# One fused decoder trunk on one core: eight weight sums in another place, a decay computed in another split, and the first weights loaded in two halves

## The chip, the core and the metric

The kernel runs on one core of a Trainium2 chip. A core has five engines with queues of their own: TensorE (PE, matrix products), VectorE (DVE), ScalarE (ACT), GpSimd (POOL) and SyncE (SP, which here only issues DMA transfers); sixteen DMA engines move data between the memory of the chip and the core's own. Each engine works through its instructions in the order of the program and waits, where it must, for the others' semaphores. The metric is the device time of one execution in microseconds, the median of several runs.

## What is computed

Two layers on a sequence of 1024 rows of width 1024, all in fp32. Layer 0 mixes the rows by a gated delta rule (8 heads of width 128, chunks), layer 1 by a state-space model; in both a memory attention runs beside the mixer, one output projection joins the two, and an MLP with squared ReLU follows. The reference, cut:

```python
for i in range(DEPTH):                      # DEPTH = 2
    if i % 2 == 0:
        mix, xq = gdn_mixer(x, gdn_w_in[j], ...)
    else:
        mix, xq = s5_mixer(x, s5_w_in[j], ...)
    cross = memory_attention(xq, mem, w_kv_mem[i])
    h = jnp.concatenate([mix, cross], axis=-1) @ w_o[i]
    x = layer_norm(DN_ALPHA * x + h, ln1_g[i], ln1_b[i])
    f = jnp.square(jax.nn.relu(x @ mlp_w1[i])) @ mlp_w2[i]
    x = layer_norm(DN_ALPHA * x + f, ln2_g[i], ln2_b[i])
```

In the delta rule the part that the change touches is the decay of a chunk, `exp(gc_i - gc_j)` below the diagonal and 0 above it, where gc is the running sum of the gates.

## The kernel before

**Products.** Every large fp32 product is three fast products (`mm3`, lines 397 to 399): each operand is split into a high part (a cast on ScalarE) and a low part (the rest, a subtraction on VectorE), and TensorE adds high*high, high*low and low*high. The small products of the delta rule run in plain fp32. In the profile `wih` and `wil` are the two parts of a weight, `xTh` and `xTl` those of x^T, and so on.

**Stages.** Up to about 30 us x^T comes in sixteen pieces of 256 KB, and the first weight (`w_in[8]`, the keys of head 0) in one load of 512 KB behind the first piece and the small gate weights `wba`; each is cast as it arrives (`load_xT`, `gdn_load_x`). From 30 to 210 us come the keys of two heads, the memory's keys and values and the memory attention. From 210 to 620 us run seven heads of the delta rule (`run`): for head h the recurrence `gdn_recur(h)` is woven into `gdn_fill(h + 1)`, the projections and the triangular inverses of the next heads. A step of the recurrence is a chain through three engines: `ks` (PE, L1452), R (DVE, L1454), `pe` (PE, L1458), e (ACT, L1460), `pS` (PE, L1464), S (DVE, L1469), and again. After half of its eight steps the output `po` is scaled: squares on ACT (L1478), a square root on POOL (L1480), the scaling `on` on ACT (L1483), and only then may `po` be written again (L1455). For every second head `gdn_inverse` puts a block of sixteen operations on VectorE (L1260 and L1262) for the inverses of the next two. From 600 to 790 us the last recurrence and the output projection run (`out_stream`: operands `so` from loads `or`, products `tm`), with the layer norm and the transposes of its rows (`block_end`: `y`, `tw`, `xB`) at the end. From 790 us the MLP: `mlp_first` with 16 pairs of blocks, and beside it (`side`) the tables of layer 1's state-space model. Then layer 1 in the same stages.

**Sums for the MLP.** The MLP's first product multiplies blocks by a scheme with seven products in place of eight, and needs sums of weight blocks. For the first four pairs of each layer the sums are made ahead: `weight_sums(i, n)` loads four 128x512 blocks, makes four sums on VectorE (`left_sums`, L640 to L643) and stores them in `wsd` (L645), from where `mlp_weights` (L696) loads them later. The same helpers serve `out_sums` and `head_sums`, for the output projection.

**Order.** The program is traced in the order of the source, and then `settle` reorders all engines by a list scheduler with its own costs: each instruction gets a due time, an engine takes what can run and is due first, and TensorE may be reordered within a reach of 40 us. Instructions made under `aside` are due at the latest 50 us after their place in the source. The number of buffers of a tag (`TAGS`: five of h5, nine of h2) bounds how early a load can be placed. `self.begin` names the last instruction that stays in the order of the source.

Of the kernel before, what the change touches and what calls it, by code (L numbers as in the profile page):

```python
# [33 lines left out]
class Trunk:  # L34
# [620 lines left out]
        for q, o in enumerate((a, d, b, c)):  # L655
            self.nc.sync.dma_start(dst[q], o)

    def weight_sums(self, i, n):

        w = [self.a["w1"][i, 2 * n + q] for q in range(2)]  # L660
        self.left_sums([w[q][:, x * HALF:(x + 1) * HALF] for q in range(2) for x in range(2)], self.wsd[i, n])

    def head_sums(self, p, tag="h5"):

# [139 lines left out]
    def mlp_first(self, i, B, ahead, side):  # L804

        held = []
        O = self.mlp_weights(i, 0, not ahead)
        for n in range(16):
            nxt = []
            self.mlp_pair(n, O, B, ahead, held, lambda: nxt.append(self.mlp_weights(i, n + 1, n + 1 >= 4) if n < 15 else None))  # L810
            O = nxt[0]
            for fb in {2: (0,), 4: (1,), 6: (2,), 8: (3,), 10: (4,), 11: (5,), 13: (6,), 15: (7,)}.get(n, ()) if side else ():
                side(fb, ("pa",) * 4)
        self.finish(held)
        self.finish(held)

# [171 lines left out]
    def load_xT(self, wba):  # L988

        nc = self.nc  # L990
        raw = self.quad(F32, "x") + self.quad(F32, "x")
        nc.sync.dma_start(raw[0][:, 0:HALF], self.a["xT"][0:P, 0:HALF])
        nc.sync.dma_start(wba, self.a["wba"])
        r0 = self.load_raw(self.a["w_in"][8], "wir")
        xT = self.new_xT()

        def take(k, h):
            s = raw[k][:, h * HALF:(h + 1) * HALF]
            hi, lo = xT[h][0][:, k, :], xT[h][1][:, k, :]
            nc.scalar.copy(hi, s)  # L1000
            nc.vector.tensor_tensor(lo, s, f32(hi), op=ALU.subtract)

        take(0, 0)
        self.begin = nc.cur_bb.bb.instructions[-1]
        w0 = tuple(self.tile("w1", [P, 1024], F32R, "wi" + q) for q in "hl")
        for c in range(2):
            c = slice(c * HALF, (c + 1) * HALF)
            nc.scalar.copy(w0[0][:, c], r0[:, c])  # L1008
            nc.vector.tensor_tensor(w0[1][:, c], r0[:, c], f32(w0[0][:, c]), op=ALU.subtract)  # L1009
        for h in range(2):  # L1010
            for k in range(KT):
                if k or h:
                    nc.sync.dma_start(raw[k][:, h * HALF:(h + 1) * HALF], self.a["xT"][k * P:(k + 1) * P, h * HALF:(h + 1) * HALF])
        nc.sync.dma_start(self.cw, self.a["cw"])
        nc.sync.dma_start(self.ng, self.a["ng"])
        nc.gpsimd.tensor_scalar(self.ng, self.ng, 0.5, None, op0=ALU.mult)
        nc.sync.dma_start(self.dsk, self.a["dskT"])
        for k in range(KT):
            for h in range(2):
                if k or h:  # L1020
                    take(k, h)
        return xT, w0

    def gdn_load_x(self):

        nc = self.nc
        wba = self.tile("h1", [P, KT * 16], F32, "wba")
        xT, w0 = self.load_xT(wba)
        wt = self.tile("h1", [P, KT, 2, 16], F32R, "wbah")
        wv = wba.rearrange("p (k c) -> p k c", k=KT)  # L1030
        nc.scalar.copy(wt[:, :, 0, :], wv)
        nc.vector.tensor_tensor(wt[:, :, 1, :], wv, f32(wt[:, :, 0, :]), op=ALU.subtract)
        ba = self.tile("h1", [P, 8, 16], F32, "ba")
        pt = self.psum("pa", "bat", (P, 8, 32))
        for h in range(2):
            ps = self.psum(("po", "sc")[h], "ba")
            for k in range(KT):
                nc.tensor.matmul(ps[:32, :], wt[:, k].rearrange("p s c -> p (s c)"), xT[h][0][:, k, :], start=k == 0, stop=False)
                nc.tensor.matmul(ps[:16, :], wt[:, k, 0, :], xT[h][1][:, k, :], start=False, stop=k == KT - 1)
            bt = self.tile("h1", [P, HALF], F32, "baT")  # L1040
            nc.vector.tensor_copy(bt[:32, :], ps[:32, :])
            for j in range(4):
                nc.tensor.transpose(pt[:, 4 * h + j, :], bt[:32, j * P:(j + 1) * P], self.ident[:32, :32])
        nc.vector.tensor_copy(ba, pt[:, :, 0:16])
        nc.vector.tensor_tensor(ba, pt[:, :, 16:32], ba, op=ALU.add)
        self.gates(ba)
        return xT, w0
# [92 lines left out]
    def decay(self, h, hf, tag):  # L1140

        nc = self.nc
        pb = self.sums(h, hf, tag)
        d = self.tile(tag, [P, 4, P], F32, "D")
        for t in range(4):
            nc.vector.scalar_tensor_tensor(d[:, t, :], pb[:, t, :], self.ngc[:, 4 * hf + t, h:h + 1], self.maskneg, op0=ALU.add, op1=ALU.add)
        nc.scalar.activation(d, d, AF.Exp)
        return d

    def gdn_keys(self, h, xT, w=None):  # L1150
# [1080 lines left out]
    def run(self):  # L2231
        nc = self.nc
        a = self.a
        d = lambda n, shape: self.dp.tile(shape, F32, tag=n, name=n)
        dsk = self.const("dsk", [P, 64])
        self.dsk, self.same = dsk[:, 0:8], dsk[:, 8:24]
        self.rouse(8)
        self.gdn_consts()
        nc.vector.tensor_reduce(self.same, self.ident.rearrange("p (g o) -> p o g", o=16), axis=AX.X, op=ALU.add)
        self.s5_scratch()  # L2240

        self.cat = d("cat0", [1536, T])
        xT, w0 = self.gdn_load_x()
        self.kTs = self.quad(F32, "kT")
        self.TT, self.qT, self.qe, self.vT, self.zs, self.outs = {}, {}, {}, {}, {}, []
        for h in range(2):
            for _ in self.gdn_keys(h, xT, (w0, None)[h]):
                pass
            for hf in range(2):
                self.gdn_keys_out(h, hf)  # L2250
        self.gdn_inverse(0)
        kv = []
        for _ in self.mem_kv(0, kv, False):
            pass
        tags = ("h4", "h3", "h2", "h2", "h2")
        fill = self.gdn_fill(0, xT, 30.0)
        self.memory_heads(xT, kv, tags, fill)
        self.mix = self.quad(F32, "mix")
        self.take(fill, 1e9)
        self.wsd = d("wsd", [2, 4, 4, P, HALF])  # L2260
        self.osd = d("osd0", [5, 4, P, HALF])
        self.wods = [d("wod0", [5, 4, P, HALF]), d("wod1", [5, 4, P, HALF])]
        sums = {"m": self.weight_sums, "o": self.out_sums, "p": self.out_sums, "h": self.head_sums}
        for h in range(7):
            for x in {0: "h0 h1", 1: "m00 m01 m02 o00", 2: "m03 o01", 3: "h2 o02 o03 m10", 4: "o04 m11", 5: "h3 m12", 6: "m13"}.get(h, "").split():
                self.aside(sums[x[0]], *map(int, x[1:]))
            fill = self.gdn_fill(h + 1, xT, 34.0 if h % 2 else 0.0)
            self.weave(self.gdn_recur(h), fill, 2.75 if h < 5 else 1.95)
            self.take(fill, 1e9)
        self.head_sums(4, "h2")  # L2270
        x = a["x"].rearrange("(n s) d -> s n d", s=8)
        y = self.rows(x)
        self.x1 = d("x1", [8, P, T])
        self.x2 = d("x2", [8, P, T])
        self.x3 = d("x3", [8, P, T])
        self.hd = d("hd", [16, 7, P, HALF])
        steps, B, ahead = self.block_end(0, y, self.x1)
        stream = iter(lambda: next(steps), None)
        self.weave(self.gdn_recur(7), stream, 2.25)
        self.take(stream, 8.0)  # L2280
        self.gdn_out_last()
        for _ in stream:
            pass
        for _ in steps:
            pass

        self.cat = d("cat1", [1536, T])
        self.osd = d("osd1", [5, 4, P, HALF])

        def u_front(xT):  # L2290
            self.s5t = self.tile("xT", [P, 4 * T], F32, "s5t")
            self.us = [self.s5_u(m, xT) for m in range(2)]
            for u in self.us:
                next(u)
                yield

        xT = self.mlp_block(0, B, ahead, self.x1, self.s5_side, self.x2, u_front)
        for u in self.us:
            next(u)
        self.s5_front(xT)  # L2300
        y = self.rows(self.x2)
        steps, B, ahead = self.block_end(1, y, self.x3)
        for _ in steps:
            pass
        self.mlp_block(1, B, ahead, self.x3, None, a["out"].rearrange("(n s) d -> s n d", s=8), None)
        self.settle(self.begin, self.nc.cur_bb.bb.instructions[-1], reach=40.0, ahead=70.0, margin=0.2, late=0.7)
# [169 lines left out]
```

## Time and profile before

| | us |
|---|---|
| median of 3 runs | 2501.73 |
| lowest, highest | 2500.79, 2506.34 |
| the profiled execution | 2501.58 |
| its span, first to last instruction | 2499.7 |
| TensorE busy in the span | 2465.4 |
| VectorE, ScalarE, GpSimd busy | 1963.5, 1286.1, 435.2 |

The profile is of one execution. Its span is 1.9 us shorter than that execution's time. An engine is busy while it has an instruction in hand; an idle time carries the name of what ended it. TensorE's instructions overlap, so two of them start closer together than one takes. The chain of waits follows the program back from the last instruction, at each step to what released it.

### The profile page before, as it was taken

To read this page: it belongs to the slowest core of one execution; us is meant where nothing else is said; L and a number is where in the kernel's file an instruction comes from. 1 tells how busy PE (TensorE), PEld (TensorE's weight loads), DVE (VectorE), ACT (ScalarE), POOL (GpSimd) and SP (SyncE) were. 2 spreads that over 40 slices of the span, in tenths; PEclk is the share of its full clock that TensorE was granted. 3 is DMA by queue.
4 is the path that set the end of the run, shared out by engine and by line. 5 is a ranking of instruction groups with operands and counts; after the bars stand their busy time and mean duration, and the time that the engine had idled before them with its cause. 6 is when DMAs were issued, how large, how long until landed. Compare 5 with 4: busy or idle time off the path is not lost.

```text
span 2499.7 us, 36835 instructions
## 1 busy us (share of the span) xinstructions
PE 2465.4 (99%) x12133; PEld 2057.0 (82%) x12133; DVE 1963.5 (79%) x3655; ACT 1286.1 (51%) x2738; POOL 435.2 (17%) x675
## 2 busy tenths in 40 slices
PE   9999999999999999999999999999999999999998
PEld 7888887888887888878888888888887888888886
DVE  8786888777778798879988967786687666578778
ACT  6555555545456566554444244564365555544442
POOL 1242333313002033212211123111021000000001
PEclk9999999999999999999999999999999999999999
DMA  6453585768754576586454489669736444674532
GB/s 224 110 171 119 140 265 141 233 183 245 258 173 155 187 234 219 178 284 234 142 161 147 153 249 312 197 224 328 255 126 210 148 144 164 228 250 129 170 104 97
DMA packets 317167, 480.63 MB, mean 192 GB/s; under 512 B 105728, under 2 KB 136656, under 8 KB 316976
## 3 DMA queue, kind: packets, MB, share of 16 engines
q1 hardware_dynamic: 289456, 423.23, 51.5%
q0 software_dynamic: 25216, 50.86, 6.9%
q10 hardware_dynamic: 2304, 4.20, 0.4%
q8 instruction: 95, 1.56, 0.2%
q14 instruction: 96, 0.79, 0.1%
HBM read 321.39 MB, written 156.73 MB: 191 GB/s over the span
## 4 chain that ended last, share of the span: by engine, by line
PE 90%; DVE 5%; DMA 2%; ACT 2%; issue 1%; POOL 1%; SPq 0%; POOLq 0%; DVEq 0%; ACTq 0%
PE q L398 7%; PE q L399 7%; PE q L397 7%; PE pA L397 4%; PE pA L399 4%; PE pA L398 4%; PE tm L397 4%; PE tm L399 4%; PE tm L398 4%; PE wi L397 3%; PE wi L398 3%; PE wi L399 3%; PE pC L399 2%; PE pC L397 2%; PE pC L398 2%; PE pB L397 2%
## 5 line engine op out<-in xcount | busy, mean ns | idle before, releaser
L397 PE MATMUL q<-wkh,hkh 128*128 128x512 f32 x784 | 306.4, 391 | 1.2 <-ACT G L1909 1.2
L398 PE MATMUL q<-wkl,hkh 128*128 128x512 f32 x784 | 305.9, 390 | 0.4 <-DVE wkl L911 0.4
L399 PE MATMUL q<-wkh,hkl 128*128 128x512 f32 x784 | 305.4, 390 | 0.0
L910 ACT CAST wkh<-wr 128x512 fp32r<-128x512 f32 x168 | 104.8, 624 | 240.0 <-PE q L398 189.4
L521 POOL TENSOR_TENSOR mv<-mv,mhalf 128x1 f32<-128x1 f32 x32 | 27.9, 873 | 858.3 <-DVE mv L515 584.2
L397 PEld LDWEIGHTS q<-wkh,hkh 128*128 128x128 f32 x784 | 147.2, 188 | 32.8 <-ACT G L1909 2.1
L398 PEld LDWEIGHTS q<-wkl,hkh 128*128 128x128 f32 x784 | 147.3, 188 | 31.0 <-DVE wkl L911 1.1
L399 PEld LDWEIGHTS q<-wkh,hkl 128*128 128x128 f32 x784 | 147.2, 188 | 30.4
L911 DVE TENSOR_TENSOR wkl<-wr,wkh 128x512 fp32r<-128x512 f32 x168 | 116.0, 690 | 67.1 <-issue 57.7
L397 PE MATMUL wi<-xTh,wih 128*128 128x512 f32 x384 | 159.4, 415 | 1.5 <-ACT wih L1008 1.5
L399 PE MATMUL wi<-xTh,wil 128*128 128x512 f32 x384 | 152.6, 397 | 0.0
L398 PE MATMUL wi<-xTl,wih 128*128 128x512 f32 x384 | 151.7, 395 | 0.0
L911 DVE TENSOR_TENSOR hkl<-hr,hkh 128x512 fp32r<-128x512 f32 x196 | 134.8, 688 | 0.0
L910 ACT CAST hkh<-hr 128x512 fp32r<-128x512 f32 x196 | 120.8, 616 | 0.1
L397 PE MATMUL tm<-so 128*128 128x512 f32 x280 | 109.8, 397 | 0.1
L1644 ACT CAST so<-or 128x1024 fp32r<-128x1024 f32 x70 | 71.8, 1049 | 69.1 <-DMA or<-wod 47.1
L1645 DVE TENSOR_TENSOR so<-or,so 128x1024 fp32r<-128x1024 f32 x70 | 84.3, 1221 | 19.5 <-ACT so L1644 19.2
L399 PE MATMUL tm<-so 128*128 128x512 f32 x224 | 88.1, 395 | 0.0
L398 PE MATMUL tm<-so 128*128 128x512 f32 x224 | 87.5, 392 | 0.0
L399 PEld LDWEIGHTS wi<-xTh,wil 128*128 128x128 f32 x384 | 72.2, 188 | 15.1 <-DVE wil L1009 0.4
L397 PEld LDWEIGHTS wi<-xTh,wih 128*128 128x128 f32 x384 | 72.5, 189 | 13.2 <-ACT wih L1008 2.1
L398 PEld LDWEIGHTS wi<-xTl,wih 128*128 128x128 f32 x384 | 72.6, 189 | 11.4
(600 smaller groups left out, 7373.3 us busy)
## 6 DMA issues: line engine op xcount, KB each, us to landing
hr<-hd SPq DMA_DIRECT2D x212, 256.0 KB, 2.7
wr<-in_w_dram SPq DMA_DIRECT2D x56, 512.0 KB, 4.9
hd<-u SPq DMA_DIRECT2D x92, 256.0 KB, 2.1
w1r<-in_w_dram SPq DMA_DIRECT2D x32, 512.0 KB, 3.5
hd<-hid SPq DMA_DIRECT2D x60, 256.0 KB, 2.3
hd<-p SPq DMA_DIRECT2D x60, 256.0 KB, 2.2
w1r<-in_w_dram SPq DMA_DIRECT2D x56, 256.0 KB, 3.5
wir<-in_w_in_dram SPq DMA_DIRECT2D x24, 512.0 KB, 4.7
```

The source lines that it names most:

```text
L397: mm(ps, a[0], b[0], start=start, stop=False, skip_group_check=onto)
L398: mm(ps, a[0], b[1], start=False, stop=False, skip_group_check=onto)
L399: mm(ps, a[1], b[0], start=False, stop=stop, skip_group_check=onto)
L521: nc.gpsimd.tensor_tensor(mv[:, 3:4], mv[:, 2:3], self.mhalf[:, 0:1], op=ALU.pow)
L910: nc.scalar.copy(hi, s)
L911: nc.vector.tensor_tensor(lo, s, f32(hi), op=ALU.subtract)
L1644: nc.scalar.copy(hi, r)
L1645: V.tensor_tensor(lo, r, f32(hi), op=ALU.subtract)
```

## The change

Four edits.

1. The weight sums of the MLP leave the seven heads. Layer 0's four (`m00` to `m03`, before beside heads 1 and 2) now stand around the recurrence of head 7 and the output projection, with buffers of tag h2 instead of h5. Layer 1's four (`m10` to `m13`, before beside heads 3 to 6) stand in layer 0's `mlp_first`, after pairs 1, 3, 12 and 14.
2. The decay: VectorE adds the mask to a whole 128x512 block in one operation instead of four of 128x128 that add mask and gate, and ScalarE takes the exponential in four operations of 128x128 with the gate as bias, instead of one of 128x512.
3. The first weight is loaded in two halves of 256 KB; pieces 1 to 3 of x^T go between them. The casts stand in the source in the order of arrival, those of the gate weights before those of the first half, and `self.begin` moves behind the first half's.
4. `load_xT` returns the cast gate weights, which `gdn_load_x` made before.

```diff
-    def weight_sums(self, i, n):
+    def weight_sums(self, i, n, tag="h5"):
 
         w = [self.a["w1"][i, 2 * n + q] for q in range(2)]
-        self.left_sums([w[q][:, x * HALF:(x + 1) * HALF] for q in range(2) for x in range(2)], self.wsd[i, n])
+        self.left_sums([w[q][:, x * HALF:(x + 1) * HALF] for q in range(2) for x in range(2)], self.wsd[i, n], tag)
...
+            if side and n in (1, 3, 12, 14):
+                self.aside(self.weight_sums, 1, (1, 3, 12, 14).index(n))
...
-        r0 = self.load_raw(self.a["w_in"][8], "wir")
+        r0 = self.tile("raw", [P, 1024], F32, "wir")
+        nc.sync.dma_start(r0[:, 0:HALF], self.a["w_in"][8][:, 0:HALF])
+        for k in (1, 2, 3):
+            nc.sync.dma_start(raw[k][:, 0:HALF], self.a["xT"][k * P:(k + 1) * P, 0:HALF])
+        nc.sync.dma_start(r0[:, HALF:], self.a["w_in"][8][:, HALF:])
...
         take(0, 0)
-        self.begin = nc.cur_bb.bb.instructions[-1]
+        wt = self.tile("h1", [P, KT, 2, 16], F32R, "wbah")
+        wv = wba.rearrange("p (k c) -> p k c", k=KT)
+        nc.scalar.copy(wt[:, :, 0, :], wv)
+        nc.vector.tensor_tensor(wt[:, :, 1, :], wv, f32(wt[:, :, 0, :]), op=ALU.subtract)
         w0 = tuple(self.tile("w1", [P, 1024], F32R, "wi" + q) for q in "hl")
-        for c in range(2):
+
+        def part(c):
             c = slice(c * HALF, (c + 1) * HALF)
             nc.scalar.copy(w0[0][:, c], r0[:, c])
             nc.vector.tensor_tensor(w0[1][:, c], r0[:, c], f32(w0[0][:, c]), op=ALU.subtract)
+
+        part(0)
+        self.begin = nc.cur_bb.bb.instructions[-1]
+        part(1)
...
         d = self.tile(tag, [P, 4, P], F32, "D")
+        nc.vector.tensor_tensor(d, pb, self.maskneg.unsqueeze(1).to_broadcast([P, 4, P]), op=ALU.add)
         for t in range(4):
-            nc.vector.scalar_tensor_tensor(d[:, t, :], pb[:, t, :], self.ngc[:, 4 * hf + t, h:h + 1], self.maskneg, op0=ALU.add, op1=ALU.add)
-        nc.scalar.activation(d, d, AF.Exp)
+            nc.scalar.activation(d[:, t, :], d[:, t, :], AF.Exp, bias=self.ngc[:, 4 * hf + t, h:h + 1])
...
-            for x in {0: "h0 h1", 1: "m00 m01 m02 o00", 2: "m03 o01", 3: "h2 o02 o03 m10", 4: "o04 m11", 5: "h3 m12", 6: "m13"}.get(h, "").split():
+            for x in {0: "h0 h1", 1: "o00", 2: "o01", 3: "h2 o02 o03", 4: "o04", 5: "h3"}.get(h, "").split():
...
+        self.aside(self.weight_sums, 0, 0, "h2")
         self.weave(self.gdn_recur(7), stream, 2.25)
+        self.aside(self.weight_sums, 0, 1, "h2")
         self.take(stream, 8.0)
+        self.aside(self.weight_sums, 0, 2, "h2")
         self.gdn_out_last()
+        self.aside(self.weight_sums, 0, 3, "h2")
```

Since the scheduler plans all engines anew, the order moves beyond these lines. TensorE's matmuls are the same 11,315 in both, and their order differs at the start, in the heads and in a few places up to about 1100 us. Three places follow, each before and in the change. In a row stand the line, the operation, what it writes and reads, and the shape; "x3" is three alike in a row. Lines of the change are numbered by its own source.

SyncE at the very start of the program (x is a piece of x^T, wba the gate weights, wir the first weight). Before:

```order
L992 DMA x_114<-in_xT_dram 128x512
L993 DMA wba_113<-in_wba_dram 128x128
L354 DMA wir_118<-in_w_in_dram 128x1024
L1013 DMA x_114<-in_xT_dram 128x512 x3
L1013 DMA x_115<-in_xT_dram 128x512 x3
```

The same queue in the change:

```order
L994 DMA x_114<-in_xT_dram 128x512
L995 DMA wba_113<-in_wba_dram 128x128
L997 DMA wir_118<-in_w_in_dram 128x512
L999 DMA x_114<-in_xT_dram 128x512 x3
L1000 DMA wir_118<-in_w_in_dram 128x512
L1027 DMA x_115<-in_xT_dram 128x512 x3
```

The weight's second half has moved behind pieces 1 to 3.

TensorE in the second half of head 5's recurrence, from `pe` of the sixth step on (near 567 us in the trace before; wi and wz are products of the projections, vt transposes of v). Before, down to `pe` of the seventh step:

```order
L1458 MATMUL pe_6213<-R_6196,iv_5176 128x128
L1464 MATMUL pS_6230<-e_6215,kdl_5887 128x128
L1470 MATMUL po_6121<-e_6215,mix_1753 128x128
L1452 MATMUL ks_6252<-S_6232,kT_289 128x128
L1455 MATMUL po_6121<-S_6232,gb_5714 128x128
L1366 MATMUL vt_6334<-ident,vT_6004 128x128 x4
L397 MATMUL wi_6410<-xTh_9_120,wih_6406 128x512
L398 MATMUL wi_6410<-xTl_10_121,wih_6406 128x512
L1458 MATMUL pe_6303<-R_6254,iv_5176 128x128
```

TensorE from the same `pe` in the change, whose line is 1468 there:

```order
L1468 MATMUL pe_6102<-R_6085,iv_5081 128x128
L1376 MATMUL vt_6106<-ident,vT_5892 128x128 x4
L397 MATMUL wz_6112<-xTh_11_126,wzh_6058 128x512
L398 MATMUL wz_6112<-xTl_12_127,wzh_6058 128x512
L399 MATMUL wz_6112<-xTh_11_126,wzl_6059 128x512
```

Work of the projections has moved in between: the next `pe` stands 28 matmuls behind this one, before 11; over the last three distances it is 27, 28 and 31, before 61, 11 and 12.

VectorE at the end of the layer norm's rows in layer 0 (near 786 us in the trace before; y and tw are rows and differences that TensorE transposes, xB the low parts of the transposes). Before:

```order
L533 SCALAR_TENSOR_TENSOR y_6911<-y_6911,mv_8306,gb_7667 128x512
L2325 TENSOR_TENSOR y_6902<-y_6910,y_6902 128x512
L2325 TENSOR_TENSOR tw_8004<-y_6911,y_6902 128x512
L545 TENSOR_TENSOR xB_8001<-xt_8352,xB_8001 128x4x128
L545 TENSOR_TENSOR xB_8002<-xt_8360,xB_8002 128x4x128
```

The same engine in the change:

```order
L533 SCALAR_TENSOR_TENSOR y_6784<-y_6784,mv_8243,gb_7604 128x512
L2339 TENSOR_TENSOR y_6775<-y_6783,y_6775 128x512
L640 TENSOR_TENSOR ws_8588<-ws_8587,ws_8588 128x512
L2339 TENSOR_TENSOR tw_7941<-y_6784,y_6775 128x512
L641 TENSOR_TENSOR ws_8587<-ws_8585,ws_8587 128x512
L545 TENSOR_TENSOR xB_7938<-xt_8289,xB_7938 128x4x128
L642 TENSOR_TENSOR ws_8585<-ws_8588,ws_8585 128x512
```

Three of the four operations of layer 1's first weight sum have moved in; the fourth stands five rows further on.

More of the change, by code (lines that the diff above doesn't have):

```diff
@@ L1009, in load_xT @@
             nc.vector.tensor_tensor(w0[1][:, c], r0[:, c], f32(w0[0][:, c]), op=ALU.subtract)
+        part(0)
+        self.begin = nc.cur_bb.bb.instructions[-1]
+        part(1)
         for h in range(2):
             for k in range(KT):
-                if k or h:
+                if k > 3 or h:
                     nc.sync.dma_start(raw[k][:, h * HALF:(h + 1) * HALF], self.a["xT"][k * P:(k + 1) * P, h * HALF:(h + 1) * HALF])
@@ L1021, in load_xT @@
                     take(k, h)
-        return xT, w0
+        return xT, w0, wt
     def gdn_load_x(self):
@@ L1027, in gdn_load_x @@
         wba = self.tile("h1", [P, KT * 16], F32, "wba")
[L1028 to L1032, printed above, removed]
+        xT, w0, wt = self.load_xT(wba)
         ba = self.tile("h1", [P, 8, 16], F32, "ba")
```

## The prediction

> **What bounds the kernel now.** I read the page's first part, then the busy time by stages of the program, then TensorE's own waits and the chain of waits in the stages where TensorE is not busy all the time. First the page, and the windows by stage (us of the window; busy time of each engine with its instructions; granted clock; DMA share; GB/s):
>
> ```profile
> span 2499.7 us, 36835 instructions
> PE 2465.4 (99%) x12133; PEld 2057.0 (82%) x12133; DVE 1963.5 (79%) x3655; ACT 1286.1 (51%) x2738; POOL 435.2 (17%) x675
> ...
> 0.00:50.00 50.00, 46.67 (x249) 36.29 (x250) 39.97 (x101) 31.02 (x69) 4.24 (x16) 1.00 0.65 222
> 50.00:250.00 200.00, 199.71 (x1095) 170.50 (x1094) 151.91 (x347) 115.89 (x331) 62.22 (x105) 1.00 0.49 140
> 250.00:600.00 350.00, 340.21 (x1911) 289.12 (x1909) 285.18 (x576) 187.05 (x596) 123.16 (x199) 1.00 0.67 195
> 600.00:750.00 150.00, 150.00 (x763) 125.61 (x762) 112.71 (x173) 78.62 (x171) 7.96 (x8) 1.00 0.68 227
> 750.00:800.00 50.00, 46.87 (x241) 37.10 (x240) 46.59 (x78) 34.93 (x79) 16.75 (x14) 1.00 0.44 151
> 800.00:1100.00 300.00, 298.39 (x1349) 246.35 (x1348) 248.53 (x571) 178.20 (x319) 71.77 (x131) 1.00 0.64 214
> 1100.00:2488.00 1388.00, 1381.65 (x6531) 1150.84 (x6530) 1070.58 (x1807) 660.37 (x1177) 146.00 (x201) 1.00 0.57 192
> ```
>
> TensorE (PE) is the bound: of 2499.7 us it is unbusy for 34.3 (2499.7 - 2465.4). The change gives it the same 11,315 matmuls in the order of the program, so the time can only move by that idle time. It lies in few places: 3.3 us in the first 50 (50 - 46.67), 0.3 up to 250, 9.8 in the seven heads of layer 0 between 250 and 600 (350 - 340.21), none in 600 to 750, 3.1 in 750 to 800, 1.6 up to 1100. Behind 1100 are 6.4 up to 2488 and the rest, 9.8, in the tail of the last layer norm; there the change has no line, and TensorE's order hardly differs.
>
> **The start.** The timeline of the first 10 us (start, us, engine, line, instruction, in brackets the idle time before it and what ended it), and the DMA share of 6.5 to 12.1 us, when only 256 KB pieces of x^T are on the way:
>
> ```profile
> 6.62 1.14 ACT L1008 CAST wih<-wir 128x512 fp32r<-128x512 f32 x2 [2.38 <-DMA wir<-in_w_in_dram]
> ...
> 7.29 0.50 PE L397 MATMUL wi<-xTh,wih 128*128 128x512 f32 x1 [1.47 <-ACT wih L1008]
> ...
> 8.02 0.19 PEld L399 LDWEIGHTS wi<-xTh,wil 128*128 128x128 f32 x1 [0.43 <-DVE wil L1009]
> ...
> 9.52 0.41 PE L1039 MATMUL ba<-xTl,wbah 128*16 128x512 f32 x1 [0.53 <-DVE xTl L1001]
> ...
> DMA packets 1288, 2.08 MB, mean 372 GB/s; under 512 B 274, under 2 KB 274, under 8 KB 1288
> ```
>
> TensorE (PEld is its weight load) waits 1.47, 0.43 and 0.53 us for the 512 KB of first weights and the pieces behind them: 2.4 us is the most that this edit can return. By SyncE's (SP's) order, shown with the change, 256 KB of the weights now go behind three pieces of x^T. At 372 GB/s 256 KB are 0.7 us, so the first half and pieces 1 to 3 land that much earlier: the floor of the gain is 0.7 us, its ceiling 2.4. VectorE (DVE) has the casts of three pieces to do before TensorE runs freely, so I take the middle: **-1.5 us**. The later pieces come as before, and TensorE consumes a piece more slowly (five matmuls) than one arrives, so nothing is given back.
>
> A rule speaks against the halves: the Trainium skill, "DMA: Bandwidth & Descriptors", section "Bandwidth", advises batching transfers to at least 1 MiB. By it two 256 KB loads would lose to one of 512 KB and the term would go to nothing; the 372 GB/s of the row above, made of 256 KB pieces alone, does not bear it out here.
>
> **The heads, 250 to 600.** Two loads leave this stage: the eight weight sums of L658 (four 512-wide VectorE operations, four loads and four stores of 256 KB each), and part of the decay. Rows of single lines (duration min/median/max in ns, first and last start):
>
> ```profile
> L640 DVE TENSOR_TENSOR ws<-ws,ws x10: 676/685/693, 297.8 to 616.5; 128x512 f32<-128x512 f32 x10
> ...
> L1146 DVE SCALAR_TENSOR_TENSOR D<-gb,scr x64: 333/347/376, 46.5 to 495.1; 128x128 f32<-128x128 f32 x64
> ...
> L1147 ACT ACTIVATE D<-D x16: 622/633/673, 47.7 to 497.3; 128x512 f32<-128x512 f32 x16
> ...
> L1177 ACT ACTIVATE kd<-kt,scr x64: 348/369/410, 46.0 to 496.1; 128x128 f32<-128x128 f32 x64
> ```
>
> Sums: 8 x 4 x 0.685 = 21.9 us of VectorE leave. Decay: per call four of 0.347 (1.4) become one 512-wide addition, like L640's 0.685, so 0.7 saved 16 times; ScalarE (ACT) pays four of about 0.37 (L1177's kind, 1.5) for one of 0.633, 0.85 more 16 times. ScalarE is busy 187 of 350 us here and VectorE 285, so the swap goes to the engine with room; on the decay's own path 0.7 less and 0.85 more cancel. I price it at nothing: its cover is that spare time; without it, 16 x 0.15 = 2.4 us at most.
>
> None of it is on TensorE, so the gain is in its waits: in 400 to 450, 450 to 550 and 560 to 575 (total, times, longest), with the window that holds the longest:
>
> ```profile
> PE po L1455 <- ACT on L1483: 2.3, 1, 2.3
> PE pS L1464 <- ACT e L1460: 1.1, 1, 1.1
> ...
> 400.00:450.00 50.00, 46.42 (x257) 39.55 (x256) 42.67 (x86) 25.37 (x83) 22.40 (x35) 0.97 0.59 164
> ...
> PE po L1455 <- ACT on L1483: 1.4, 1, 1.4
> PE pS L1464 <- DMA kdl<-kdd: 1.0, 1, 1.0
> PE pS L1464 <- ACT e L1460: 0.4, 1, 0.4
> ...
> PE ks L1452 <- DVE S L1469: 0.9, 1, 0.9
> PE pe L1458 <- DVE R L1454: 0.8, 1, 0.8
> PE pS L1464 <- ACT e L1460: 0.7, 2, 0.4
> ```
>
> *At 531*: the chain of waits there, with the one at 495:
>
> ```profile
> 486.78 5.01 DMA gb<-gcd
> ...
> 495.13 1.06 ACT on L1483 x4
> ...
> 496.23 0.49 PE po L1455 x2
> ...
> 525.55 0.29 DVE ws L643
> 525.93 0.27 SPq L645
> 526.28 6.07 DMA kdl<-kdd
> ...
> 532.40 0.49 PE pS L1464 x2
> ```
>
> A sum (L643) holds its store on SP's queue (L645), and the load of kdl stands behind that store: the 1.0 us wait is the sums' doing and goes: -1.0. At 495 a load of 5.0 us heads the chain, among the sums' loads; of the 1.4 I take -0.9.
>
> *At 566*: the recurrence of head 5 is issued faster than its chain runs. By TensorE's order, shown with the change, the last three distances from pe (L1458) to pe go from 61, 11 and 12 matmuls to 27, 28 and 31: the waits of the last group (0.9, 0.8 and 0.7) should nearly vanish: -2.2. *At 428 to 439*: the inverse's 16 VectorE operations stand between steps 0 and 1 of head 3 instead of 1 and 2, its tight distances go from 20 and 15 matmuls to 20 and 21, and POOL's square root of the output norm (L1480) no longer stands behind four stores of N^T. The waits are 2.3 + 1.1, and the clock granted in that window is 0.97, so 1.5 us of 50 were lost behind them: of 4.9 in all I take -2.8. New tight steps (14 and 18 matmuls at head 5's start, against 17 and 28) may cost +1.0. **Heads: -5.9**; bounds -11.3 (9.8 idle and 1.5 of clock) and, with the decay's 2.4 uncovered and nothing won, +2.4.
>
> The clock has a rule: the Trainium skill, "TensorE: Matmul & The Clock Gate", section "What's actually happening", has it halve after an idle window of about 3.4 us. The trace halves it with single waits of 2.3 and 1.1 us, so shorter idleness suffices here; by the rule none of the changed gaps brings it back, which is also what my sum has.
>
> **Where the sums go.** Layer 0's four stand at 640 to 697, in the output projection, layer 1's first at 772 to 794 and the next three at 808 to 825, about 1000 to 1028 and 1045 to 1072 (the times are those that their neighbours in the order have in the trace before). Windows of the first two places, and TensorE's waits in 775 to 800:
>
> ```profile
> 640.00:697.00 57.00, 57.00 (x289) 48.03 (x289) 40.46 (x57) 25.74 (x52) 2.02 (x2) 1.00 0.66 212
> 775.00:800.00 25.00, 21.87 (x112) 16.42 (x111) 22.62 (x39) 16.16 (x37) 8.13 (x7) 1.00 0.64 217
> ...
> PE xt L540 <- DVE xB L545: 0.8, 2, 0.6
> PE pA L397 <- ACT p L624: 0.7, 1, 0.7
> PE pA L399 <- DVE w1l L364: 0.5, 1, 0.5
> PE pB L397 <- DVE xB L545: 0.5, 1, 0.5
> ```
>
> At 640 VectorE has 16.5 us free of 57 and gets 16 x 0.685 = 11.0 more; the DMA engines, busy 0.66, get 32 x 256 KB = 8.4 MB, 147 GB/s on top of 212. It fits, with little to spare, and the stores stand on SP ahead of the projection's loads, as at 531. TensorE waited for nothing there. Bounds 0 and 5.6 (four groups at the 1.4 us of the longest wait at 495); nearer to nothing: **+0.8**.
>
> At 775 to 800 VectorE has 2.4 us free of 25, TensorE waits for it, and one sum's four operations are placed in the middle (VectorE's order, shown with the change). Three of the four stand ahead of casts (xB) and of a difference (tw), for which TensorE waits. At most 4 x 0.685 = 2.7, at least 0; half: **+1.3**. The other three fall where TensorE idles 1.6 us in 300: nothing; their cover is VectorE's 51 us free there.
>
> **Sum**: -1.5 - 5.9 + 0.8 + 1.3 = -5.3. The profiled execution took 2501.6 us (span 2499.7 and 1.9 around it), 0.1 from the median of the runs, 2501.73. Forecast: 2501.6 - 5.3 = **2496.3 us**, its own range 2493 to 2500.
>
> **Rivals.** *The heads keep their stalls.* For it: of the waits named, only the one at 531 leads back to a sum; the inverse and the recurrence stay. Against: the wider steps of head 5. Heads -2 instead of -5.9: 2500.2, no measurable change. *All comes.* Start at 2.4, three quarters of 11.3 in the heads, nothing given back: 2501.6 - 2.4 - 8.5 = 2490.7. For it: VectorE falls from 285 to about 260 us of 350 (seven sums, 19.2, and eight decays, 5.6); against: the order had slack only in places. *Slower: SP blocked in the output projection.* A store of a sum that waits for VectorE holds up the loads of the projection's operands, since SP issues in order. It decides once a load comes later than TensorE's work in hand, then each of four groups costs 1.4: +5.6, layer norm at its ceiling +2.7, heads -3 and start -1.5: 2501.6 + 3.8 = 2505.4. Against: TensorE has no wait there now.
>
> **How the numbers follow.** About 0.2%, 5 us, is what a measurement here can tell from no change. Forecast 0.48, heads kept 0.20, all 0.17, slower 0.15. The forecast's bulk lies about the 5 us line: 0.29 of its 0.48 is faster by more, 0.19 within. Faster 0.29 + 0.17 = 0.46; same 0.19 + 0.20 = 0.39; slower 0.15. Range 2488.5 to 2505.0: from a little under the "all" case to just inside the slower one.
>
> **What would show it.** First weights' cast near 5.5 instead of 6.62, TensorE's waits before 10 us under 1 in sum; 250 to 600 with 343 us or more busy in 350, no kdl load behind a store of sums, clock 1.00 in 400 to 450; 640 to 697 still full; 775 to 800 with a little more idle. Wrong, if TensorE waits for so or tm in 640 to 700, or if new waits of the recurrence arise elsewhere in the heads.

## The result and the profile after

| | before | after |
|---|---|---|
| median, us | 2504.46 (22 runs, 2499.72 to 2509.33) | 2499.14 (22 runs, 2494.07 to 2504.15) |
| the profiled execution, us | 2501.58 | 2497.56 |
| its span, us | 2499.7 | 2495.9 |

The ratio of the runs is 0.9981, 95% interval 0.9975 to 0.9987: 4.8 us less (3.3 to 6.3). That is just under the 0.2%, or 5 us, that a single measurement here can tell from no change; the interval of these runs leaves no change out. The forecast was 5.3 less. (The kernel before was run again beside the others of this study, so its median has moved from the 2501.73 of three runs.)

The page of the changed kernel, and its busy time by stages (us of the window; busy time of each engine with its instructions; granted clock; DMA share; GB/s):

```profile
span 2495.9 us, 36864 instructions
PE 2464.2 (99%) x12133; PEld 2057.8 (82%) x12133; DVE 1958.1 (78%) x3607; ACT 1298.7 (52%) x2786; POOL 438.0 (18%) x675
...
0.00:50.00 50.00, 47.18 (x249) 36.63 (x250) 38.70 (x96) 31.85 (x72) 3.79 (x16) 1.00 0.66 223
50.00:250.00 200.00, 198.93 (x1089) 170.19 (x1088) 150.68 (x317) 120.61 (x350) 61.52 (x105) 1.00 0.50 138
250.00:600.00 350.00, 345.74 (x1964) 296.07 (x1963) 273.04 (x548) 197.39 (x642) 124.79 (x200) 1.00 0.59 166
600.00:750.00 150.00, 149.16 (x743) 124.44 (x743) 120.76 (x179) 77.60 (x161) 8.02 (x8) 1.00 0.71 242
750.00:800.00 50.00, 45.83 (x233) 36.62 (x232) 45.66 (x78) 32.78 (x71) 18.55 (x14) 1.00 0.66 217
800.00:1100.00 300.00, 297.88 (x1344) 245.38 (x1343) 255.28 (x585) 181.81 (x323) 71.31 (x131) 1.00 0.69 234
1100.00:2484.20 1384.20, 1377.51 (x6513) 1147.14 (x6513) 1065.86 (x1799) 656.67 (x1168) 146.91 (x200) 1.00 0.58 191
```

TensorE (PE) is unbusy for 31.7 us of the span instead of 34.3. By stage: the heads, 250 to 600, have 4.26 unbusy instead of 9.79: 5.5 less, more than the whole gain. The start has 2.82 instead of 3.33. Everything else is a little worse: 50 to 250 by 0.8, the output projection by 0.8, the layer norm (750 to 800) by 1.0, the rest by some 0.8. The remaining 1.2 of the 3.8 us by which the spans differ are busy time.

TensorE's waits of the changed kernel in 400 to 450 and 450 to 550 (total, times, longest); in 550 to 600 it has none:

```profile
PE ot L1504 <- DVE sp L1337: 1.6, 1, 1.6
PE vt L1376 <- ACT jk L1354: 0.2, 1, 0.2
...
PE ks L1462 <- DVE S L1477: 0.9, 1, 0.9
PE po L1465 <- ACT on L1493: 0.4, 1, 0.4
```

The wait for kdl and the whole group at 566 are gone. In 400 to 450 a new wait of 1.6 for `sp`, an operation of the inverse, stands where 2.3 and 1.1 stood.

### The profile page after: what moved, and what is told of

The parts are those of the page before. It is cut to its first block, busy times and chain, and to the rows that moved or that the text cites. A ratio compares the mean times of both kernels' runs of the same rounds, so it can differ in the third digit from the quotient of the medians.

```text
span 2495.9 us, 36864 instructions
## 1 busy us (share of the span) xinstructions
PE 2464.2 (99%) x12133; PEld 2057.8 (82%) x12133; DVE 1958.1 (78%) x3607; ACT 1298.7 (52%) x2786; POOL 438.0 (18%) x675
## 4 chain that ended last, share of the span: by engine, by line
PE 85%; DVE 6%; issue 3%; DMA 2%; ACT 2%; POOL 1%; SPq 0%; POOLq 0%; DVEq 0%; ACTq 0%
PE q L398 7%; PE q L397 7%; PE q L399 7%; PE pA L399 4%; PE pA L397 4%; PE pA L398 4%; PE tm L398 3%; PE tm L397 3%; PE tm L399 3%; PE wi L397 3%; PE wi L399 3%; PE wi L398 3%; PE pC L399 2%; PE pC L397 2%; PE pC L398 2%
```

## The experiments

Each ran in five rounds beside the kernel before; the us behind a ratio are its distance from 1 times the median of before in those rounds. Line numbers in their rows are those of the kernel in question and differ by some lines.

### One edit at a time, planned anew

The first weights in halves alone:

```diff
-        r0 = self.load_raw(self.a["w_in"][8], "wir")
+        r0 = self.tile("raw", [P, 1024], F32, "wir")
+        nc.sync.dma_start(r0[:, 0:HALF], self.a["w_in"][8][:, 0:HALF])
...
-        self.begin = nc.cur_bb.bb.instructions[-1]
...
+        part(0)
+        self.begin = nc.cur_bb.bb.instructions[-1]
+        part(1)
```

> The kernel before with the first weights in two halves alone. The prediction's term: 1.5 us less, with TensorE unbusy under 2 us in the first 50. By the trace of the changed kernel, where TensorE is unbusy for 2.8 of the first 50 us against 3.3 before: 0.5 us less, with the second piece of x^T landing near 7.8 us as it does there. A rival, that any edit makes the planner lay out all that follows anew and that this alone makes the 4.8 us: the unbusy time in 250 to 600 falls from 9.8 to 6 or less here too, and the whole changes by 3 us or more.

Ratio 1.0029 (1.0018 to 1.0041): 7.3 us longer, which no expectation had. The rival, a new layout of all that follows, had the size (3 us or more) but not the sign: it named a gain in the heads. The windows of 0 to 50, 250 to 600 and 750 to 800 of this kernel, with the clock below 1 in all three:

```profile
0.00:50.00 50.00, 45.99 (x235) 35.74 (x236) 38.16 (x97) 30.11 (x67) 3.78 (x16) 0.97 0.66 217
250.00:600.00 350.00, 338.98 (x1872) 288.03 (x1870) 281.49 (x571) 184.88 (x584) 120.28 (x191) 0.98 0.65 191
...
750.00:800.00 50.00, 47.12 (x235) 38.17 (x233) 45.47 (x73) 32.90 (x73) 18.49 (x15) 0.97 0.34 120
```

The heads, which this edit does not touch, have 11.0 us unbusy instead of 9.8 and four steps of 3.4 us at half clock instead of one (what a step is stands in the last section). Over the whole program, the tail aside, it is six steps instead of one, and TensorE is busy for 6.1 us more (2471.5 against 2465.4).

Layer 0's four sums alone, and behind them layer 1's alone. The cut shows layer 0's; for layer 1's, `m10` to `m13` leave the same table and the two lines in `mlp_first` come in, as in the whole change.

```diff
-            for x in {0: "h0 h1", 1: "m00 m01 m02 o00", 2: "m03 o01", ...
+            for x in {0: "h0 h1", 1: "o00", 2: "o01", ...
...
+        self.aside(self.weight_sums, 0, 0, "h2")
         self.weave(self.gdn_recur(7), stream, 2.25)
...
```

> The kernel before with layer 0's four weight sums alone moved out of heads 1 and 2 into the output projection; layer 1's stay in heads 3 to 6. By the prediction: the waits at 428 to 439 (head 3's start) may go, the recurrence of head 5 at 566 and the wait at 531 stay, since layer 1's sums still stand there; 640 to 697 costs 0.8. In all 0 to 2 us less. If it is the sums as a load on VectorE wherever they stand, half of them give half of the heads' 5.5: 2.8 less, 0.8 given back, 2 us less. If the order that the planner finds makes it: anything between 4 us less and 2 us more, with unbusy time in places that have nothing to do with a sum.

Ratio 1.0023 (1.0014 to 1.0033): 5.8 us longer. The heads improve (5.9 unbusy), the output projection gives back 1.7, but the loss is elsewhere. The window of 800 to 1100, TensorE's waits in it, and what VectorE waited for just ahead (970 to 990):

```profile
800.00:1100.00 300.00, 291.84 (x1312) 240.78 (x1311) 241.42 (x557) 175.81 (x313) 66.44 (x124) 0.99 0.60 202
...
PE pA L399 <- DVE a1l L590: 8.2, 4, 3.6
...
DVE co L1873 <- DMA co<-in_c_dram: 4.8, 1, 4.8
```

VectorE stands 4.8 us before an operation for layer 1's tables whose transfer has not landed, and `a1l`, which the MLP needs, is queued behind it. No sum has a part in this wait: the new order has that operation ahead of its data.

> The kernel before with layer 1's four weight sums alone moved out of heads 3 to 6 into the first pass of layer 1's feed-forward; layer 0's stay. By the prediction: the wait for kdl at 531 (1.0) and head 5's recurrence at 566 (2.2) go, the layer norm costs 1.3 more: 2 to 3 us less in all, with 450 to 600 full and 775 to 800 at 4.2 us unbusy of 50 as in the changed kernel. If each sum counts alike: 2.8 less in the heads and 1.0 given back in the layer norm, 1.8 less. If the order alone decides: between 4 less and 2 more.

Ratio 0.9996 (0.9987 to 1.0005): 1.0 less, not to be told from nothing. Its parts went the way that the prediction said: 450 to 600 has 0.9 unbusy instead of 5.1, and 750 to 800 has 5.1 instead of 3.1, which is 2.0 more where 1.3 was named.

The decay alone:

```diff
+        nc.vector.tensor_tensor(d, pb, self.maskneg.unsqueeze(1).to_broadcast([P, 4, P]), op=ALU.add)
         for t in range(4):
-            nc.vector.scalar_tensor_tensor(d[:, t, :], pb[:, t, :], self.ngc[:, 4 * hf + t, h:h + 1], self.maskneg, op0=ALU.add, op1=ALU.add)
-        nc.scalar.activation(d, d, AF.Exp)
+            nc.scalar.activation(d[:, t, :], d[:, t, :], AF.Exp, bias=self.ngc[:, 4 * hf + t, h:h + 1])
```

> The kernel before with the decay's new split alone (one sum on VectorE and four exponentials on ScalarE instead of four and one). By the prediction nothing: within 0.5 us, and no more than 2.4 us longer if ScalarE has no cover. A rival, that VectorE's load in the heads is what counts and 5.6 us of it go here in 250 to 600: 1 to 1.5 us less by the heads' 5.5 for some 25 us of VectorE. If the order alone decides: between 4 less and 2 more.

Ratio 0.9996 (0.9987 to 1.0004): nothing, as predicted.

These four add up to +11.1 us (7.3 + 5.8 - 1.0 - 1.0), the whole change gives -4.8. Prices that belong to the edits would add. What does not add is either the edits acting on each other or the order, which the planner lays out anew for all engines after any edit; the next runs hold the order.

### The edits with the order kept

So the planner's choice was replaced by a table: the total order that it had found for the kernel before (or for the changed one), and of what may run the instruction that comes first in the table.

```diff
-                        k = (0, due[x] + other, r, x) if r <= free[e] + 0.1 else (1, r + other, due[x], x)
+                best_x = min((x for e in names for x in open_[e] if not fresh[x] or room(x) is not None), key=lambda x: rank_[x])
...
```

TensorE's order is then that of the kernel in the table, but for one instruction at most, and on the other engines hardly any but the instructions of the edit move. The moved sums stand between 630 and 720 us and from 880 us on.

> The first weights in halves alone, all else in the order of the kernel before. Planned anew, this edit alone was 7 us slower. If that was the edit: 7 us slower here too, with half-clock spells about 500, 572 and 784 again. If it was the order: the start's own worth only, between 1.5 less (the prediction's term) and 0.5 more (a second piece of x^T that lands at 7.8 us instead of 7.6).

Ratio 1.0008 (0.9999 to 1.0017): 2.0 longer (0.3 less to 4.3 more). So some 5 of the 7.3 were order. And the edit itself is worth nothing, or costs something. TensorE's waits in the first 14 us:

```profile
PE ba L1033 <- ACT xTh L991: 2.3, 1, 2.3
PE z L945 <- DVE cv L1113: 1.1, 1, 1.1
PE wi L384 <- ACT wih L1003: 1.0, 1, 1.0
PE ba L1033 <- DVE wbah L998: 0.4, 1, 0.4
```

The wait for the weights falls from 1.5 to 1.0 and one of 2.3 for the second piece of x^T takes its place.

> All eight weight sums at their new places, all else in the order of the kernel before. By the prediction's terms without the recurrence's new distances: -1.0 at 531, -0.9 at 495, +0.8 in the output projection, +1.3 in the layer norm: 0 to 1 us less. If the sums' load on VectorE and SP is what stalls the heads: 3 to 4 us less, with under 6 us unbusy in 250 to 600.

Ratio 1.0197 (1.0183 to 1.0211), 49 us longer, and the most telling run of all. In the heads, where sums were only taken away, the windows of 400 to 450, 450 to 550 and 550 to 600, and the waits in them:

```profile
400.00:450.00 50.00, 46.41 (x256) 39.50 (x255) 42.19 (x88) 24.71 (x84) 22.39 (x36) 0.97 0.60 166
450.00:550.00 100.00, 99.64 (x568) 85.20 (x568) 74.00 (x155) 56.25 (x183) 25.99 (x42) 1.00 0.59 168
550.00:600.00 50.00, 47.60 (x273) 40.49 (x273) 40.58 (x76) 21.93 (x64) 23.41 (x41) 1.00 0.68 195
...
PE po L1444 <- ACT on L1472: 2.3, 1, 2.3
PE pS L1453 <- ACT e L1449: 1.1, 1, 1.1
...
PE pS L1453 <- ACT e L1449: 0.4, 1, 0.4
...
PE ks L1441 <- DVE S L1458: 0.9, 1, 0.9
PE pe L1447 <- DVE R L1443: 0.8, 1, 0.8
PE pS L1453 <- ACT e L1449: 0.7, 2, 0.4
```

Read against the rows of before: 400 to 450 and 550 to 600 are the same, wait for wait. Between them, 450 to 550 goes from 2.75 unbusy to 0.36; the 1.4 for `on` and the 1.0 for kdl are gone and the 0.4 stays. In 250 to 400 a wait of 0.4 for `jk` is gone too. So the whole of the heads goes from 9.8 to 7.0.

How large these three waits are differs from execution to execution. The run before this one, the start alone in the order of before, has all its sums in the heads and the same order there. The row of `jk` in the kernel before, then the three rows of that run:

```profile
PE vt L1366 <- ACT jk L1344: 0.4, 1, 0.4
...
PE vt L1361 <- ACT jk L1339: 1.4, 1, 1.4
...
PE po L1450 <- ACT on L1478: 0.7, 1, 0.7
PE pS L1459 <- DMA kdl<-kdd: 0.2, 1, 0.2
```

The three make 2.8 us in the kernel before and 2.3 there, with 9.8 and 9.6 unbusy in the whole of the heads. So the sums were the cause of these three waits, some 2.5 us together, and the size of a single one is not to be relied on.

The loss begins where the sums went. The windows of 600 to 750 and 800 to 1100, VectorE's timeline at 650 (start, us, engine, line, instruction, idle time before it and what ended it), and what TensorE waited for in 640 to 653:

```profile
600.00:750.00 150.00, 137.20 (x667) 112.81 (x666) 102.72 (x153) 67.16 (x146) 6.06 (x6) 0.95 0.71 235
800.00:1100.00 300.00, 279.58 (x1227) 227.04 (x1228) 234.91 (x536) 164.81 (x298) 65.28 (x116) 0.97 0.63 210
...
650.80 0.69 DVE L627 TENSOR_TENSOR ws<-ws,ws 128x512 f32<-128x512 f32 x1 [5.96 <-DMA ws<-in_w_dram]
651.40 0.34 DVE L1443 SCALAR_TENSOR_TENSOR R<-ks,scr,mix 128x128 f32<-128x128 f32 x1
...
PE pe L1447 <- DVE R L1443: 5.3, 1, 5.3
```

12.8 and 20.4 us are unbusy. A sum waits 6.0 us for its blocks, the recurrence's R stands behind it, and TensorE waits 5.3. That is the prediction's slower rival, with the engine changed (VectorE holds the queue, SP only delivers late): it comes true when the other instructions cannot be placed around the sums. In 800 to 1100 a sum waits 9.3 us for its blocks in the same way, ahead of 884.6. Another 17.5 us are busy time (2482.9 against 2465.4), with 13 steps at half clock in place of one.

> All of the change, but the planner's choice is replaced by a table: every instruction that both kernels have stands on its engine as in the kernel before, and only the changed ones (sums, decay, first loads) stand at their new places. If the edits themselves make the 4.8 us: 4 to 5 us less than before. If the order that the planner found for the changed program makes it: within 2 us of before, with the waits of the recurrence at 566 still there, since its distances are those of before.

Ratio 1.0246 (1.0232 to 1.0260), 62 longer, with the loss in the same two stages (15.2 and 23.2 unbusy); in the heads 7.3 unbusy, of which 2.4 in 550 to 600 as before. The waits for `jk` and kdl are gone here too; of the one for `on` 0.6 is left, with the decay moved as well.

> The kernel before, none of the change made, but every instruction that both kernels have stands in the order of the changed kernel; the sums stay in the heads. If the order makes the gain: 3 to 5 us less than before, with the recurrence's waits at 566 gone. If the edits make it: within 1.5 us of before.

Ratio 1.0285 (1.0271 to 1.0299), 71 longer. Both expectations missed: the order of the changed kernel has no room for the eight sums in its heads. The window of 250 to 600, and VectorE's longest wait in it, again for the blocks of a sum, here of one for the output projection, which both kernels have in the heads:

```profile
250.00:600.00 350.00, 297.04 (x1585) 248.84 (x1584) 242.71 (x503) 159.84 (x508) 97.57 (x156) 0.92 0.58 165
...
DVE ws L639 <- DMA ws<-in_w_o_dram: 17.1, 3, 6.1
```

So neither plan serves the other program, and these runs price only what they take away, not what they put in.

### Two parts, and other orders

The changed kernel with one edit undone, and both kernels with another constant in the planner:

```diff
-        self.settle(self.begin, self.nc.cur_bb.bb.instructions[-1], reach=40.0, ahead=70.0, margin=0.2, late=0.7)
+        self.settle(self.begin, self.nc.cur_bb.bb.instructions[-1], reach=40.0, ahead=71.0, margin=0.2, late=0.7)
```

> The changed kernel with the decay's split undone, planned anew: start and sums remain. If the decay is worth nothing by itself, as predicted: within 1 us of the changed kernel, 4 to 6 us less than before. If the changed kernel's gain is one lucky order among many: anywhere between 6 us less and 7 us more than before.

Ratio 0.9995 (0.9986 to 1.0004): 1.3 less than before, 3.5 above the changed kernel, though the decay is worth nothing alone.

> The changed kernel with the start undone, planned anew: sums and decay remain. If the prediction's sum of terms holds: 1.5 us above the changed kernel, 3 less than before. If the start costs 1 us by itself, as in the order of before: 1 us below the changed kernel, 6 less than before. If the order decides: anywhere between 6 less and 7 more.

Ratio 0.9994 (0.9985 to 1.0003): 1.5 less than before, 3.3 above the changed kernel, though the start alone gains nothing. Both are near the edge of what can be told, and fit neither prices that add nor a fixed gain of the sums.

> The kernel before with nothing changed but one constant of the planner (how far ahead of its due time work may be placed, 71 us instead of 70), which gives another order of the same instructions. If orders of one program are worth the same within 1 us: 0. If the order alone moves the time as the single edits did: some 2 to 7 us, of either sign.

Ratio 0.9999 (0.9990 to 1.0007): 0.3 less.

> The changed kernel with the same constant of the planner at 71 instead of 70. If the gain belongs to the edits, whatever the order: 4 to 6 us less than before. If it belongs to this one order: back within 2 us of before, or slower.

Ratio 0.9985 (0.9976 to 0.9994): 3.8 less. Within their intervals (1.5 to 6.0 less here) the gain survives this other order, and the old program does not find it in its other one. The heads of these two, in the same sequence:

```profile
250.00:600.00 350.00, 345.57 (x1934) 293.81 (x1932) 288.75 (x586) 188.82 (x596) 122.86 (x199) 0.99 0.68 196
```

```profile
250.00:600.00 350.00, 346.12 (x1971) 295.94 (x1971) 271.94 (x549) 196.18 (x639) 123.54 (x200) 1.00 0.58 166
```

The old program can have 4.4 unbusy there too with all its sums in place. Its profile then has 1.5 more in 800 to 1100 and four stretches at half clock instead of one, and its time does not move. So less idle time in the heads alone does not make a faster kernel. No version beat the changed kernel; its second order cannot be told from it.

## Why the prediction was right, and where it was wrong

**The number.** 5.3 less was forecast, 4.8 measured (3.3 to 6.3), 4.0 between the two profiled executions (2501.58 - 2497.56). The bound was read rightly, and the gain came where it was said to come, in TensorE's idle time in the heads. That the sum came so near is in part luck. The start gave 0.5 in the profile where 1.5 stood, and 1.6 us of loss in 50 to 250 and behind 800 stand at nothing in the sum; 1.2 us less of busy time, which the sum has at nothing too, made up for part of it. "The time can only move by that idle time" was too narrow: the start alone, planned anew, changed the busy time by 6.1 us.

**Heads, -5.9.** 5.5 us less unbusy, and 345.7 busy where 343 was named. The split holds by parts. The waits at 495 and 531 were given to the sums (-1.9 together); taking the sums away and nothing else makes 450 to 550 lose 2.4 against the kernel before, but 0.9 against the other run in the same order (1.28 unbusy there). The 2.2 at 566 were given to the new distances of the recurrence: in the order of before they stay to 0.1, sums or no sums, and in the new order they are gone. So this part is the order's. At 428 to 439 only 1.8 of the expected 2.8 came: the wait for `sp` is new, and the clock stays at 0.97 where 1.00 was forecast. The 1.0 for new tight steps is there as the 0.9 of `ks`, at 534 us in the second step of head 5.

**Start, -1.5.** This step failed: "the first half and pieces 1 to 3 land that much earlier: the floor of the gain is 0.7 us". The first half did come earlier here, the pieces did not. The changed kernel's first 9 us, and what its DMA engines moved in 2 to 12 us:

```profile
5.39 0.62 ACT L1018 CAST wih<-wir 128x512 fp32r<-128x512 f32 x1 [0.99 <-DMA wir<-in_w_in_dram]
...
7.84 1.87 ACT L1006 CAST xTh<-x 128x512 fp32r<-128x512 f32 x3 [1.83 <-DMA x<-in_xT_dram]
...
8.52 0.42 PE L1048 MATMUL ba<-xTh,wbah 128*32 128x512 f32 x1 [1.23 <-ACT xTh L1006]
...
DMA packets 1915, 3.05 MB, mean 305 GB/s; under 512 B 334, under 2 KB 462, under 8 KB 1915
```

The cast of the second piece and the same DMA row of the kernel before:

```profile
7.67 1.79 ACT L1000 CAST xTh<-x 128x512 fp32r<-128x512 f32 x3
...
DMA packets 1892, 3.26 MB, mean 326 GB/s; under 512 B 334, under 2 KB 462, under 8 KB 1892
```

The weights' cast is at 5.39 as named, but the second piece of x^T is cast at 7.84, before at 7.67, and TensorE waits 1.2 for it. Without the first 1.1, which both kernels have, its waits before 10 us are 1.5 in sum, where under 1 was named. The early cast is in part luck: over the profiles it begins at 4.92 to 6.61 us with halves and at 5.26 to 6.71 with the load in one. The 372 GB/s from which the floor was worked out is that of a stream in full run; in 2 to 12 us the halves bring less. Over all profiles: the six with halves moved 2.85 to 3.05 MB in these 10 us (mean 3.00) and left TensorE unbusy for 2.5 to 4.8 of the first 20 (mean 3.7), the seven with the load in one 3.09 to 3.32 MB (3.19) and 2.2 to 3.7 (3.0); one kernel, whose TensorE waits there for something else, is left out. The difference is all ahead of 6.5 us (0.92 to 1.08 MB against 1.05 to 1.26); from 6.5 to 12 us both move 1.93 to 2.08. 0.19 MB at 372 GB/s are 0.5 us. So the edit is worth nothing, with some sign of a loss; why the pieces behind the first half come no earlier, no run shows. The Trainium skill, "DMA: Bandwidth & Descriptors", section "Bandwidth", advises batching transfers to at least 1 MiB. By it the term would go to nothing, and here it did, with 3.00 MB against 3.19; the prediction set the rule aside by a row from later in the stream.

**Where the sums go, +0.8 and +1.3.** The output projection has 0.84 more unbusy, the layer norm 1.04 more. TensorE's waits in 600 to 750 and the longest group in 750 to 800:

```profile
PE po L1465 <- ACT on L1493: 0.6, 1, 0.6
PE tm L397 <- ACT so L1654: 0.2, 1, 0.2
...
PE xt L540 <- DVE xB L545: 2.8, 4, 1.1
```

The 2.8 for `xB` stood at 0.8 in the rows of before: the sum's operations ahead of it on VectorE, as named. In the projection the wait for `so` is only 0.2, at 639 us, just ahead of the 640 to 700 in which it would have been a sign of being wrong; the rest is head 7's recurrence.

**Sums later, 0.** 0.5 more in 800 to 1100 and 0.3 behind: small, but not nothing.

**Decay, 0.** Right: 1.0 less alone, with nothing inside its interval.

**What the sum left out.** All terms were worked out from one pair of orders, and in this pair they hold but for the start. One place had none: 50 to 250 loses 0.8, by a wait of 1.0 for ScalarE (`ct`) that the start alone, planned anew, has too (0.9). The terms are not prices of edits. Start alone, forecast at -1.5, gave +7.3, and layer 0's sums +5.8, for the most part at places that neither touches. The rival that "the heads keep their stalls" had its point: the sums by themselves account for 2.7 to 2.8 of the 5.5 there (250 to 600 goes from 9.8 or 9.6 to 7.0 unbusy in the order of before). For the rest the new order is left; it was not seen by itself, since the kernel before in the order of the changed one, which was to show it, lost more to its sums.

**Open.** Why the full change gets a better plan than any part of it, and whether its parts act on each other. Two orders of each program are too few to say how far orders of one program spread, and one profile of each kernel is too few for differences between stages of under 1 us.

## What to carry to other kernels

In a program that a list scheduler lays out, an edit's effect is its own price and a new draw of the order, and here the draw was the larger; the parts of a change must be measured with the order kept, and then only what is taken away is priced fairly. A sum or copy that is moved is safe only if its inputs have landed when its engine reaches it: on an in-order engine everything behind it waits too. At the start of a program, take the rate of the stream from the first microseconds, not from a later stretch.

## What the runs showed of the hardware

TensorE's clock was granted in steps of 3.41 us on a fixed grid. All stretches at half clock in these profiles (but the one in the tail) last 3.41 us or a multiple of it and, within one execution, lie whole numbers of steps apart: in the kernel with the start alone 125, 144, 165 and 227 steps behind the first. Three steps of the changed kernel, in order of time (the clock is the third number from the end):

```profile
440.80:444.20 3.40, 1.60 (x10) 0.99 (x10) 2.04 (x4) 2.47 (x7) 3.20 (x6) 1.00 0.94 260
444.20:447.60 3.40, 3.40 (x15) 3.01 (x14) 3.19 (x8) 0.58 (x1) 0.55 (x1) 0.50 0.99 251
447.60:451.00 3.40, 3.40 (x20) 2.95 (x20) 2.27 (x5) 0.63 (x2) 2.17 (x4) 1.00 1.01 347
```

In the first TensorE is busy for 1.60 of 3.40 us, and the next step runs at half clock. Over the fourteen profiles, between 12 and 2470 us, steps at full clock with TensorE busy for under 1.5 us were followed by half clock in 33 of 33 cases, with 1.5 to 1.94 us in 7 of 26, with 1.94 to 2.8 in none of 155. So in these runs a wait of 2 us can halve the clock or not by where it falls on the grid: inside one step it leaves 1.4 us of work, shared by two steps it can leave 2.4 in each. At the granted clock of 0.50 a step costs up to 1.7 us (an estimate, half of its 3.41 us). The Trainium skill, "TensorE: Matmul & The Clock Gate", section "What's actually happening", has a free-running window of 3.4 us, with which the trace agrees, and has the clock halve after an idle window; here a step that was busy for up to 1.5 us was always enough.
